# Hybrid trunk kernel: the forget cumulative sums move behind the k projection of the fox branch's first head

## The chip, the cores and the metric

One Trainium2 chip, of which the kernel uses one core. The metric is the device time of one execution in microseconds (us); lower is better. The engines are TensorE (PE in the profile), VectorE (DVE), ScalarE (ACT), GpSimd (POOL) and SyncE (SP), which here issues most DMA transfers. Each engine takes its instructions in the order in which they stand in its own queue, and waits for semaphores that other engines or transfers raise.

## The reference

Two layers over a sequence of 512 rows of width 1024. Each layer is a half-step SwiGLU, then three token mixers in parallel (stick-breaking attention, forgetting attention, cross-attention to a memory of 256 rows), then a second half-step SwiGLU. What matters here is the forgetting ("fox") branch with 8 heads of width 64:

```python
u = _rmsnorm(h, mix_pre_g[l])
proj = u @ w_in[l]
q_sb, k_sb, v_sb, q_fx, k_fx, v_fx, f_logit, q_mem = jnp.split(proj, split_at, axis=-1)
log_f = jax.nn.log_sigmoid((f_logit + b_forget[l]).astype(jnp.float32)).transpose(0, 2, 1)
...
def _forgetting_attention(q, k, v, log_f):
    c = lax.cumsum(log_f.astype(jnp.float32), axis=2)
    ...
        z = jnp.einsum('bhqd,bhkd->bhqk', qb, k).astype(jnp.float32) * scale
        z = z + cb[..., :, None] - c[..., None, :]
        ...softmax over the causal keys, times v
```

So each head's scores get a bias from the running sum `c` of its log forget gates, one number per row and head.

## The kernel before

Matrix products are made of three products of split numbers (`mm3`, lines 205 to 207: high by high, high by low, low by high), 128 x 128 weights against 512 columns, accumulated in PSUM. A weight block is a `Unit`: SP fetches it into a `raw_` buffer (line 249; there are two such buffers), ACT casts the high part `wh_` from it (line 179, or 182 with a scale), DVE subtracts to get the low part `wl_` (line 180 or 183), which frees the raw buffer for the next fetch. There are four places for `wh_` and four for `wl_`. All names below have a layer and head number in the code; the profile leaves the numbers out.

The work of a layer's mixing stage is a queue of jobs (`Q.add`). Each job names the units that it needs, and a generator that issues matmuls piece by piece. When a job begins, its units and at least four of those of the jobs behind it are loaded (`load_ahead`). The attention heads are chains that are woven into the jobs: `weave` issues the pieces of jobs until an assumed time has passed, then the chain's next step. So between the matmuls of the projections stand a head's scores (`zs`, line 1153), its transposes (`pts`, line 1128) and its product with the values (`pvs`, line 1114). The stick-breaking heads come first: between `zs` and `pts`, ACT and DVE make the weights `ts` (lines 1158 to 1168, of which line 1168 is the last exponential on ACT). All instructions of an engine then stand in a fixed order, which a scheduler makes from this program order and its own estimate of times.

PSUM has eight banks in two rings of four. The ring `mm` serves the projections: `pv` (values), `pq` and `pk` (q and k of a pair of heads), `pg` (gates), `pb` (branch products), `pvs`, and `pfl`, which is the bank of the forget sums.

The fox branch begins with the head pair `FOX[0]`, which is pair 2, while the stick-breaking heads of pair 2 still run. Its jobs are:

- `v_gates`: the values of the pair and, in eight more columns, the forget logits. For each of four row tiles PE fills a bank `pv`, ACT and DVE split the values out of it, and DVE copies the eight logit columns to `fl` (line 1334).
- the q projection (`proj`): 24 matmuls into `pq`, then a split by ACT and DVE.
- `forget_cumsum`: PE transposes the four tiles of `fl` into `pfl` (line 1283); ACT and DVE make the log-sigmoid and the running sum (a scan, line 1290); ACT, DVE and POOL place it in four row groups of the tile `cs` (lines 1293 to 1296).
- the k projection: 24 matmuls into `pk`, then a split, and two copies on POOL (line 1362).
- a `merge` job of the memory branch: the gate product `pg`, its sigmoid (lines 193 to 201), the branch product `pb`.

`cs` is read by `fox_pre` (line 1188), which builds the bias operand `qk` of each fox head.

Of the kernel before, what the change touches and what calls it, by code (L numbers as in the profile page):

```python
# [22 lines left out]
def kernel(  # L23
# [1250 lines left out]
    FOX = (2, 3, 0, 1)  # L1274

    def forget_cumsum(l, fl, holder):

        pt = pbank("mm", f"pfl{l}")
        for t in range(NT):
            tc.keep_in_program_order(nc.tensor.transpose(pt[:NH, t * P:(t + 1) * P], fl[:, t], ident[:]))
        yield 0.3
        a, b, y = tmp(f"fa{l}")[:NH], tmp(f"fb{l}")[:NH], bfor[:, l:l + 1]
        nc.scalar.activation(a, pt[:NH], AF.Abs, bias=y)
        nc.scalar.activation(a, a, AF.Exp, scale=-1.0)
        nc.scalar.activation(a, a, AF.Ln, bias=one_t[:NH])
        nc.vector.tensor_scalar(b, pt[:NH], y, 0.0, ALU.add, ALU.min)
        nc.vector.tensor_tensor_scan(b, b, a, 0.0, ALU.add, ALU.subtract)  # L1290
        cs = stile([P, S], "cs", f"cs{l}")
        nc.gpsimd.memset(cs[:].bitcast(F32), 0.0)
        nc.scalar.copy(cs[0:NH], b)
        nc.vector.tensor_tensor(cs[32:32 + NH], b, cs[0:NH].bitcast(F32), ALU.subtract)
        for c in (0, 32):
            nc.gpsimd.tensor_copy(cs[64 + c:64 + c + NH], cs[c:c + NH])
        holder["cs"] = cs

    def mixing(l, src, ks, vs, rest, dst):
# [44 lines left out]
        def proj(key, un, scale):  # L1344
            nm = f"{key[0]}{l}_{key[1]}_{key[2]}"
            pt = pbank("mm", "p" + nm)
            yield from gemm(pt[:], [un], 0, act)
            if key[0] == "q":

                t = st[key] = blk("q", nm)  # L1350
                for r, ro, j in HEAD_ROWS:
                    split(t[r, j], t[ro, j], pt[r], scale=scale)
            else:

                twice = key[1] == 0
                t = st[key] = stile([P, 4 if twice else 3, S], "k", nm)
                for r, ro, j in HEAD_ROWS:
                    split(t[r, j], t[r, 2 + j if twice else 2], pt[r])
                    if twice:
                        nc.gpsimd.tensor_copy(t[ro, j::2], t[r, j::2])  # L1360
                    else:
                        nc.gpsimd.tensor_copy(t[ro, j], t[r, j])
# [12 lines left out]
        def project(br, p):  # L1375
            base = br * 1536
            marks["before", br, p] = len(Q.jobs)
            for x, off, scale in (("q", 0, 0.125), ("k", 512, None)):
                un1 = Unit(w_in[l], 0, ND, base + off + p * P, P, f"{x}{l}_{br}_{p}")
                marks[br, p] = Q.add([un1], lambda x=x, un1=un1, scale=scale: proj((x, br, p), un1, scale))  # L1380
                if (br, p, x) == (1, FOX[0], "q"):
                    Q.add([], lambda: forget_cumsum(l, st["fl"], st))

        def merge(br, w_br, dp, apart=False, saved=False):
# [58 lines left out]

        heads, fox = [(0, p) for p in range(NP)] + [(1, p) for p in FOX], []
        project(*heads[0])
        project_v(*heads[0])
        marks[heads[0]] = len(Q.jobs)
        for i, (br, _) in enumerate(heads):
            if i + 1 < len(heads):
                project(*heads[i + 1])  # L1450
            if br == 0:
                merge(2, w_br_mem, i)
            else:
                merge(0, w_br_sb, i - NP, apart=i == NP)
            if i % 2 == 0 and i + 2 < len(heads):
                project_v(*heads[i + 2])
            if i in (1, 3):
                fox.append(merge(1, w_br_fox, i // 2, True, True))
# [239 lines left out]
```

## Time and profile before

| | |
|---|---|
| time, median of three runs | 2399.95 us (2398.45 to 2400.62) |
| profiled execution: time | 2400.15 us |
| profiled execution: span of the instructions | 2398.4 us |
| PE busy | 2375.6 us, 99% of the span |
| DVE busy | 1862.4 us, 78% |
| ACT busy | 1392.5 us, 58% |
| POOL busy | 78.4 us, 3% |
| DMA | 338.22 MB, mean 141 GB/s |

The span runs from the first to the last instruction; the profiled execution's time has 1.75 us around it. A busy PE is not a PE at its peak: the profile also gives the clock that was granted to it (PEclk), as a share of full speed. In the views a row of the timeline is: start and duration in us, engine, line, operation, tile written <- tiles read, shape, count, and in brackets the idle time of the engine before it and what ended that.

### The profile page before, as it was taken

The page shows a single profiled execution, that of the slowest core. Times are in us where ns is not written, and L with a number is a line of the kernel's source. Part 1 is how long each engine was busy: PE and PEld are TensorE (multiplying, and loading weights), DVE is VectorE, ACT ScalarE, POOL GpSimd, SP SyncE. Part 2 cuts the span into 40 slices and gives each one's busy share as a digit, 9 for nine tenths or more (in the row PEclk, how much of TensorE's full clock was granted, in tenths as well). Part 3 has the DMA queues.
Part 4 walks back from the last instruction along what each step waited for, and adds up shares of the span by engine and source line. Part 5 has one row for each costly group of instructions (what it writes and reads, how often), then busy time and mean ns, then how long its engine had stood idle before and what let it go on. Part 6 is the DMA issues. An engine that isn't in the chain of part 4 may idle for free.

```text
span 2398.4 us, 31561 instructions
## 1 busy us (share of the span) xinstructions
PE 2375.6 (99%) x11975; PEld 2009.8 (84%) x11975; DVE 1862.4 (78%) x2462; ACT 1392.5 (58%) x2201; POOL 78.4 (3%) x134
## 2 busy tenths in 40 slices
PE   9999999999999999999999999999999999999998
PEld 7788889888888888888888888888888888888887
DVE  8878877577777789788788788766667777887885
ACT  6655565576656555555655554655666664655554
POOL 1000000000111000000000000000001100000000
PEclk9999999999999999999999999999999999999999
DMA  5654454222323555544645554532323235555444
GB/s 200 187 150 158 141 194 140 80 82 78 88 80 99 192 181 170 150 150 158 210 138 170 149 175 162 188 107 71 97 71 97 71 122 191 164 182 149 154 139 155
DMA packets 232171, 338.22 MB, mean 141 GB/s; under 512 B 10682, under 2 KB 125394, under 8 KB 232020
## 3 DMA queue, kind: packets, MB, share of 16 engines
q1 hardware_dynamic: 231924, 336.18, 44.3%
q8 instruction: 94, 1.54, 0.3%
q14 instruction: 57, 0.47, 0.1%
q0 software_dynamic: 96, 0.03, 0.0%
HBM read 319.39 MB, written 16.78 MB: 140 GB/s over the span
## 4 chain that ended last, share of the span: by engine, by line
PE 94%; DVE 3%; DMA 1%; ACT 1%; issue 1%; POOL 0%; DVEq 0%; SPq 0%; ACTq 0%
PE pg L206 4%; PE pg L205 4%; PE pg L207 4%; PE pda L206 3%; PE pda L207 3%; PE pda L205 3%; PE pdc L206 3%; PE pdc L207 2%; PE pdc L205 2%; PE pb L207 2%; PE pb L206 2%; PE pb L205 2%; PE pk L205 1%; PE pk L206 1%; PE pk L207 1%; PE pwo L206 1%
## 5 line engine op out<-in xcount | busy, mean ns | idle before, releaser
L205 PE MATMUL pg<-us_a,wh_wg 128*128 128x512 f32 x384 | 150.8, 393 | 0.0
L206 PE MATMUL pg<-us_a,wh_wg 128*128 128x512 f32 x384 | 149.6, 390 | 0.0
L207 PE MATMUL pg<-us_a,wl_wg 128*128 128x512 f32 x384 | 149.6, 390 | 0.0
L206 PE MATMUL pdc<-wl_dc,ahc 128*128 128x512 f32 x224 | 87.6, 391 | 0.1
L206 PE MATMUL pda<-wl_da,aha 128*128 128x512 f32 x224 | 87.6, 391 | 0.0
L205 PE MATMUL pda<-wh_da,aha 128*128 128x512 f32 x224 | 87.4, 390 | 0.0
L205 PE MATMUL pdc<-wh_dc,ahc 128*128 128x512 f32 x224 | 87.4, 390 | 0.0
L207 PE MATMUL pdc<-wh_dc,alc 128*128 128x512 f32 x224 | 87.2, 389 | 0.0
L207 PE MATMUL pda<-wh_da,ala 128*128 128x512 f32 x224 | 87.2, 389 | 0.0
L207 PEld LDWEIGHTS pg<-us_a,wl_wg 128*128 128x128 f32 x384 | 72.1, 188 | 15.2
L205 PEld LDWEIGHTS pg<-us_a,wh_wg 128*128 128x128 f32 x384 | 72.1, 188 | 14.1
L206 PEld LDWEIGHTS pg<-us_a,wh_wg 128*128 128x128 f32 x384 | 72.2, 188 | 14.0
L180 DVE TENSOR_TENSOR wl_dc<-raw_dc,wh_dc 128x1024 fp32r<-128x1024 f32 x50 | 61.2, 1224 | 29.1 <-ACT wh_dc L179 28.5
L180 DVE TENSOR_TENSOR wl_da<-raw_da,wh_da 128x1024 fp32r<-128x1024 f32 x50 | 61.2, 1224 | 22.0 <-ACT wh_da L179 21.7
L179 ACT CAST wh_dc<-raw_dc 128x1024 fp32r<-128x1024 f32 x50 | 52.7, 1054 | 43.8 <-PE pdc L207 14.9
L179 ACT CAST wh_da<-raw_da 128x1024 fp32r<-128x1024 f32 x50 | 52.7, 1054 | 38.7 <-PE pda L207 14.5
L183 DVE SCALAR_TENSOR_TENSOR wl_wg<-raw_wg,wh_wg 128x1024 fp32r<-128x1024 f32 x48 | 58.4, 1221 | 20.4 <-ACT wh_wg L182 20.1
L179 ACT CAST wh_uc<-raw_uc 128x1024 fp32r<-128x1024 f32 x44 | 46.3, 1053 | 41.9 <-PE pwc1u L207 10.3
L182 ACT ACTIVATE wh_wg<-raw_wg 128x1024 fp32r<-128x1024 f32 x48 | 50.6, 1057 | 28.0 <-PE pv L1089 12.6
L179 ACT CAST wh_ua<-raw_ua 128x1024 fp32r<-128x1024 f32 x44 | 46.2, 1052 | 34.5 <-PE pwa1u L207 10.3
L180 DVE TENSOR_TENSOR wl_uc<-raw_uc,wh_uc 128x1024 fp32r<-128x1024 f32 x44 | 53.7, 1221 | 13.0 <-ACT wh_uc L179 12.9
L180 DVE TENSOR_TENSOR wl_ua<-raw_ua,wh_ua 128x1024 fp32r<-128x1024 f32 x44 | 53.6, 1220 | 10.2 <-ACT wh_ua L179 10.2
(654 smaller groups left out, 8028.8 us busy)
## 6 DMA issues: line engine op xcount, KB each, us to landing
raw_da<-in_ffn_w_down_dram SPq DMA_DIRECT2D x66, 512.0 KB, 4.5
raw_dc<-in_ffn_w_down_dram SPq DMA_DIRECT2D x66, 512.0 KB, 4.9
raw_ga<-in_ffn_w_gate_dram SPq DMA_DIRECT2D x52, 512.0 KB, 3.8
raw_ua<-in_ffn_w_up_dram SPq DMA_DIRECT2D x52, 512.0 KB, 3.9
raw_gc<-in_ffn_w_gate_dram SPq DMA_DIRECT2D x52, 512.0 KB, 3.7
raw_uc<-in_ffn_w_up_dram SPq DMA_DIRECT2D x52, 512.0 KB, 3.7
raw_wg<-in_w_gate_dram SPq DMA_DIRECT2D x48, 512.0 KB, 3.5
raw_wo<-in_w_out_dram SPq DMA_DIRECT2D x24, 512.0 KB, 3.6
```

The source lines that it names most:

```text
L179: both = [nc.scalar.copy(h_ap, src)]
L180: make = lambda: nc.vector.tensor_tensor(l_ap, src, h_ap.bitcast(F32), ALU.subtract)
L182: both = [nc.scalar.activation(h_ap, src, AF.Copy, scale=scale)]
L183: make = lambda: nc.vector.scalar_tensor_tensor(l_ap, src, scale, h_ap.bitcast(F32), ALU.mult, ALU.subtract)
L205: nc.tensor.matmul(pt, lh, rh, start=start, stop=False, skip_group_check=free)
L206: nc.tensor.matmul(pt, lh, rl, start=False, stop=False, skip_group_check=free)
L207: nc.tensor.matmul(pt, ll, rh, start=False, stop=stop, skip_group_check=free)
```

## The change

The job `forget_cumsum` of each layer is put into the queue after the k projection of the fox branch's first head pair instead of after its q projection. Computation, tiles and transfers are the same; their order differs.

```diff
             for x, off, scale in (("q", 0, 0.125), ("k", 512, None)):
                 un1 = Unit(w_in[l], 0, ND, base + off + p * P, P, f"{x}{l}_{br}_{p}")
                 marks[br, p] = Q.add([un1], lambda x=x, un1=un1, scale=scale: proj((x, br, p), un1, scale))
-                if (br, p, x) == (1, FOX[0], "q"):
+                if (br, p, x) == (1, FOX[0], "k"):
                     Q.add([], lambda: forget_cumsum(l, st["fl"], st))
```

`marks[br, p]`, the place up to which the queue must have run before the pair's head begins, is taken before that line in both kernels.

## The prediction

> **What bounds the kernel now.** I read the page first: the busy shares, and the chain of work that ended last.
>
> ```profile
> PE 2375.6 (99%) x11975; PEld 2009.8 (84%) x11975; DVE 1862.4 (78%) x2462; ACT 1392.5 (58%) x2201; POOL 78.4 (3%) x134
> ...
> PE 94%; DVE 3%; DMA 1%; ACT 1%; issue 1%; POOL 0%; DVEq 0%; SPq 0%; ACTq 0%
> ```
>
> TensorE (PE) is busy for 99% of the span and is 94% of the chain, so only time in which PE stands still, or runs slowly, can be won. The second view is therefore the waits of PE alone.
>
> ```profile
> engine line waited for: us in total, times, longest us
> PE pfl L1283 <- DVE fl L1334: 9.0, 2, 4.5
> PE warm L1558 <- DVE warm L1650: 1.3, 1, 1.3
> ```
>
> Its longest wait is the one that the change touches: twice, once in each layer, the transposes of the forget logits (`pfl`, line 1283) wait 4.5 us for VectorE's (DVE's) copies of those logits (`fl`, line 1334). The third view is the timeline of the first of the two, engine by engine: PE, then DVE, then ScalarE (ACT).
>
> ```profile
> 577.50 0.39 PE L205 MATMUL pq<-us_a,wh_q 128*128 128x512 f32 x1
> ...
> 582.97 0.38 PE L1283 MATMUL pfl<-ident,fl 128*8 128x128 f32 x2
> 587.87 0.38 PE L1283 MATMUL pfl<-ident,fl 128*8 128x128 f32 x1 [4.52 <-DVE fl L1334]
> 587.90 0.77 PE L205 MATMUL pk<-us_a,wh_k 128*128 128x512 f32 x1
> ...
> 595.08 1.25 PE L1128 MATMUL pts<-ident,ts 128*128 128x128 f32 x10
> 596.09 0.48 PE L205 MATMUL pk<-us_a,wh_k 128*128 128x512 f32 x1
> ...
> 596.86 0.39 PE L205 MATMUL pg<-us_a,wh_wg 128*128 128x512 f32 x1
> ```
> ```profile
> 578.34 1.20 DVE L180 TENSOR_TENSOR wl_k<-raw_k,wh_k 128x1024 fp32r<-128x1024 f32 x1
> ...
> 586.51 1.23 DVE L180 TENSOR_TENSOR wl_wb<-raw_wb,wh_wb 128x1024 fp32r<-128x1024 f32 x1 [0.18 <-ACT wh_wb L179]
> 587.65 0.16 DVE L1334 COPY fl<-pv 128x8 f32<-128x8 f32 x1
> ...
> 588.06 0.16 DVE L1334 COPY fl<-pv 128x8 f32<-128x8 f32 x1
> ```
> ```profile
> 585.43 1.04 ACT L179 CAST wh_wb<-raw_wb 128x1024 fp32r<-128x1024 f32 x1 [0.38 <-DMA raw_wb<-in_w_br_mem_dram]
> 586.38 0.52 ACT L1168 ACTIVATE ts<-ts 128x384 f32<-128x384 f32 x1
> ```
>
> The q projection `pq` ends its issue at 582.97, and two of the four transposes run. The third needs the copy at 587.65. That copy reads a PSUM bank that PE filled long before; it is late because DVE takes its instructions in order and the low part of a weight unit (`wl_wb`, 586.51) stands ahead of it. That one waits for ACT's cast of the unit (585.43), which waits for the unit's transfer, and the chain of waits gives this transfer's own time:
>
> ```profile
> 580.70 4.71 DMA raw_wb<-in_w_br_mem_dram
> ```
>
> So PE stands still for a weight that only a later job needs. The second layer does the same at 1772.10:
>
> ```profile
> 1772.10 0.38 PE L1283 MATMUL pfl<-ident,fl 128*8 128x128 f32 x2
> 1776.93 0.38 PE L1283 MATMUL pfl<-ident,fl 128*8 128x128 f32 x1 [4.46 <-DVE fl L1334]
> ...
> 1785.33 0.39 PE L205 MATMUL pg<-us_a,wh_wg 128*128 128x512 f32 x1
> ```
>
> The fourth view cuts both places into stretches, with the granted clock in the last but two columns.
>
> ```profile
> core 0: us, PE busy (x) PEld busy (x) DVE busy (x) ACT busy (x) POOL busy (x), PEclk, DMA share, GB/s
> ...
> 587.87:596.86 8.99, 8.99 (x36) 7.16 (x37) 5.47 (x10) 4.66 (x10) 1.67 (x2) 0.74 0.32 97
> ...
> 1776.93:1785.33 8.40, 8.40 (x37) 6.76 (x37) 5.47 (x10) 4.67 (x10) 1.66 (x2) 0.80 0.34 105
> ```
>
> Behind each standstill PE is busy without a gap, but its mean granted clock is 0.74 and 0.80. The k projection pays for the wait a second time.
>
> **The change part by part.** It moves the whole job `forget_cumsum` behind the k projection in the queue. Nothing is added or removed.
>
> PE. In the built order of the changed program the 24 matmuls of `pk` follow `pq` directly, then come the ten transposes `pts`, then all four `pfl`, then `pg`. Can `pk` start at 582.97? It needs a PSUM bank: it takes the one that `pfl` had, and since two `pfl` ran at 582.97, that bank was free. It needs its weights: `wl_k`, the later of the two parts, ended at 578.34 + 1.20 = 579.54. So nothing holds it. The 24 matmuls of `pq` took 582.97 - 577.50 = 5.47 us at the full clock, and 24 of `pk` take the same: 588.44. `pts` needs the last exponential, over at 586.38 + 0.52 = 586.90; its cost is 596.09 - 595.08 = 1.01, so 589.45. `pfl` needs the last `fl` copy, over at 588.06 + 0.16 = 588.22. This is the cover that counts: the copies are as late as before, but the k projection and `pts` now hide them, with 1.23 us to spare. Four `pfl` at some 0.11 us each (ten `pts` transposes in 1.01, nearly the same shape) end at 589.9, and `pg` starts there instead of at 596.86: 6.96 us won. In the second layer the same 6.93 us of work leads from 1772.10 to 1779.03 instead of 1785.33: 6.30 us. The sum is 13.3 us. Of it 4.52 + 4.46 = 9.0 us is standstill, and the other 4.3 us is nearly all the low clock.
>
> On this clock the Trainium skill ("TensorE: Matmul & The Clock Gate", Part 1, "What's actually happening") says that an idle window of about 3.4 us halves the clock and a busy window of about 3.4 us restores it, with windows that run freely. By that rule alone each standstill costs 1.7 us more, and the sum would be an estimated 12.4 us. The trace agrees on the kind (4.5 us idle, then a low clock) and gives 0.9 us more in all.
>
> DVE, ACT and POOL. The job's own chain (three activations, two DVE steps and a scan, one cast, two POOL copies) keeps its place relative to `pfl` and so comes some 2 us later than before. Its result `cs` is read much later, as the first of these rows (the tile `cs` as a whole) shows; some 45 us of room hide it:
>
> ```profile
> L1188 DVE TENSOR_SCALAR qk<-cs,sel x16: 457/481/669, 641.3 to 1947.0; 40x512 fp32r<-40x512 f32 x8, 64x512 fp32r<-64x512 f32 x8
> L1296 POOL CAST cs<-cs x4: 608/831/1057, 594.1 to 1784.3; 8x512 fp32r<-8x512 f32 x4
> ```
>
> POOL's order changes only in that its two k copies come ahead of the `cs` copies. The job issues no DMA. SP's queue here keeps the order of its weight transfers.
>
> What is late next. The seven idle microseconds were also time in which ACT and DVE caught up. In the built order the job's chain now meets the gate and attention chains of the following job, and ACT casts the next k unit (`wh_k`) *ahead* of the last exponential (line 1168) that the next `pts` needs. In the profile of before the exponential comes first:
>
> ```profile
> 615.71 0.51 ACT L1168 ACTIVATE ts<-ts 128x384 f32<-128x384 f32 x1
> 616.13 0.67 ACT L193 ACTIVATE ga<-pg,nbgate 128x512 f32<-128x512 f32 x1
> 617.46 1.05 ACT L179 CAST wh_k<-raw_k 128x1024 fp32r<-128x1024 f32 x1 [0.66 <-DMA raw_k<-in_w_in_dram]
> ```
> ```profile
> 603.59 0.62 PE L1153 MATMUL zs<-k,q 128*128 128x512 f32 x2
> ...
> 612.41 1.22 DVE L183 SCALAR_TENSOR_TENSOR wl_wg<-raw_wg,wh_wg 128x1024 fp32r<-128x1024 f32 x1
> ...
> 613.66 0.37 SPq L249 DMA_DIRECT2D raw_k<-in_w_in_dram  x1
> ...
> 619.17 1.25 PE L1128 MATMUL pts<-ident,ts 128*128 128x128 f32 x10
> ```
>
> So a wait is added: the last exponential, and behind it PE's `pts`, stand behind the transfer `raw_k`, which SP may start only when `wl_wg` (612.41) has freed its place. Before, `raw_k` was issued 613.66 - 603.59 = 10.07 us after the scores `zs` began. In the changed order `zs` begins at 589.9 + (603.59 - 596.86) + 0.68 (three matmuls of `pb` come ahead of it) = 597.3, so the issue is at 607.4 at best. The transfer takes 617.46 - 613.66 = 3.80, the cast 1.05, the exponential 0.51: 612.8. PE reaches those transposes 619.17 - 596.86 + 0.68 = 22.99 us after `pg`, at 612.9. That is even at best; with a step or two of the job's displaced chain (0.6 to 0.7 us each on ACT or DVE) ahead of `wl_wg`, PE waits. I take 0.5 us per layer, between 0 and 1.5. Below nothing it cannot be, since PE has no idle time there now to win.
>
> The sum: 13.3 - 1.0 = 12.3 us. The profiled execution took 2400.15 us, of which 2398.4 is the span; the 1.75 us around it stay. It lies 0.2 us above the median of the three runs (2399.95, from 2398.45 to 2400.62). 2400.15 - 12.3 = 2387.9 us.
>
> **The rivals.** *Partly given back.* The wait at `pts`, or one at the moved `pfl` (1.23 us of room behind a transfer that took 4.71), is longer than I take, but shorter than the 4.5 us that are seen to cost clock. For it speaks that both stand behind transfers; against it, that this stage's transfers, 3.80 and 4.71 us, are priced already. With up to 3.3 us per layer: 2386.9 + 6.6 = 2393.5 us at most. Chance 0.14.
>
> *It does not do what it says.* Something else than `fl` holds PE until 587.65, and `pk` inherits the wait: a bank, or a weight. Then PE stands as before, and the time is 2400 us. Against it: the rows for `wl_k` and for the two `pfl` at 582.97. Chance 0.05.
>
> *Slower.* The transfer `raw_k` becomes the bound of the stage: ACT stands behind it, then `pts`, then the whole next head. It loses more than was won from a wait of 4.5 us per layer on, because a standstill of that length is seen to bring the low clock with it (6.3 to 7.0 us each); that needs a transfer of 8 us. It is slower by 0.2%, that is over 2405 us, with some 9 us, of which 7 stand and 2 are clock; at 7.5 us of standstill it gives 2386.9 + 2 x 9.5 = 2406 us. The order of ACT's queue speaks for it, the two transfer times against it. Chance 0.04.
>
> **How the numbers follow.** The forecast, 2387.9 us, has the remaining 0.77, and lies between 2386.9 (no new wait) and 2389.9 (1.5 us per layer), to which run-to-run scatter of 1.7 us below the profiled execution is added: 2385.2. The range from 2385.0 to 2393.5 takes in the first rival and leaves out 0.09 of named cases. About 0.2%, 4.8 us, is what a measurement of this kernel can tell from no change; faster than that (under 2395.1) are the forecast and the first rival, 0.91; the second rival is the same, 0.05; the third is slower, 0.04.
>
> **What would show it.** In the profile of the changed kernel the wait of `pfl` on `fl` is gone from PE's waits, `pk` runs in some 5.5 us at a granted clock of 1.0, and `pg` follows `pq` after some 6.9 us in both layers. A new line `pts` behind line 1168, of up to a microsecond or so, is the term that I am least sure of. I am wrong if `pk`'s first matmul shows the old wait, if any PE wait of over 3.3 us appears in the heads behind it, or if the granted clock still drops there.

## The result and the profile after

The changed kernel takes 2388.56 us (median of four executions, 2386.77 to 2389.78) where the kernel before takes 2400.28 us on the same chip (2398.45 to 2400.86): a ratio of 0.9953, with a 95% interval from 0.9938 to 0.9968. Run again later on another chip it took 2390.96 us against 2401.22 us: 0.9956, from 0.9944 to 0.9969. That is 11.7 us won the first time and 10.3 the second. The forecast was 2387.9 us, in a range from 2385.0 to 2393.5. The profiled execution took 2388.54 us, 2386.8 us of it the span. One execution of experiment 4 below took 11399 us and is left out of its ratio.

From the page after, the busy shares and the chain of work that ended last:

```profile
PE 2370.1 (99%) x11975; PEld 2007.1 (84%) x11975; DVE 1862.3 (78%) x2462; ACT 1392.1 (58%) x2201; POOL 74.9 (3%) x134
...
PE 91%; DVE 4%; DMA 2%; ACT 1%; issue 1%; SPq 0%; POOL 0%; DVEq 0%; ACTq 0%
```

The counts of instructions are the same. What is new is in the chain: three points less of PE, one more each of DVE and of the transfers (the shares are rounded). The waits of PE say where (us in total, times, longest):

```profile
PE pts L1128 <- ACT ts L1168: 1.5, 2, 0.9
```

The 9.0 us at `pfl` are gone; in their place stand 1.5 us at `pts`, once in each layer. The timeline of PE in the first layer, then that of DVE and ACT:

```profile
582.23 0.39 PE L205 MATMUL pk<-us_a,wh_k 128*128 128x512 f32 x1
...
587.68 1.26 PE L1128 MATMUL pts<-ident,ts 128*128 128x128 f32 x10
588.77 0.60 PE L1283 MATMUL pfl<-ident,fl 128*8 128x128 f32 x4
...
612.23 0.49 PE L1128 MATMUL pts<-ident,ts 128*128 128x128 f32 x3
613.27 0.98 PE L1128 MATMUL pts<-ident,ts 128*128 128x128 f32 x7 [0.55 <-ACT ts L1168]
```
```profile
585.50 1.22 DVE L180 TENSOR_TENSOR wl_wb<-raw_wb,wh_wb 128x1024 fp32r<-128x1024 f32 x1
...
587.04 0.16 DVE L1334 COPY fl<-pv 128x8 f32<-128x8 f32 x1
...
611.75 1.05 ACT L179 CAST wh_k<-raw_k 128x1024 fp32r<-128x1024 f32 x1 [2.13 <-DMA raw_k<-in_w_in_dram]
612.70 0.52 ACT L1168 ACTIVATE ts<-ts 128x384 f32<-128x384 f32 x1
```

The copies `fl` come as late as before, behind `wl_wb` on DVE, but PE now does `pk` and ten `pts` in the meantime and needs the last copy only at 588.77, 1.57 us after it is done. Further on, ACT casts `wh_k`, for whose transfer it waited 2.13 us, ahead of the exponential, and PE waits 0.55 us for that. In the second layer the same wait is 0.94 us:

```profile
1796.93 0.98 PE L1128 MATMUL pts<-ident,ts 128*128 128x128 f32 x7 [0.94 <-ACT ts L1168]
```

Cut into stretches, from the first `pk` to the first `pg` in either layer (busy time of each engine, then the granted clock):

```profile
582.23:589.13 6.90, 6.90 (x39) 5.82 (x38) 6.21 (x13) 4.67 (x7) 0.00 (x0) 1.00 0.55 167
1765.51:1772.41 6.90, 6.90 (x40) 5.82 (x38) 5.75 (x13) 4.03 (x7) 0.00 (x0) 1.00 0.55 167
```

Both take 6.90 us at a clock of 1.00, where the way from the end of `pq` to `pg` took 13.89 and 13.23 us. So 6.99 + 6.33 = 13.3 us are won and 1.5 lost: 11.8 us. The spans differ by 2398.4 - 2386.8 = 11.6 us.

### The profile page after: what moved, and what is told of

The parts are those of the page before. It is cut to its first block, busy times and chain, and to the rows that moved or that the text cites. A ratio compares the mean times of both kernels' runs of the same rounds, so it can differ in the third digit from the quotient of the medians.

```text
span 2386.8 us, 31552 instructions
## 1 busy us (share of the span) xinstructions
PE 2370.1 (99%) x11975; PEld 2007.1 (84%) x11975; DVE 1862.3 (78%) x2462; ACT 1392.1 (58%) x2201; POOL 74.9 (3%) x134
## 4 chain that ended last, share of the span: by engine, by line
PE 91%; DVE 4%; DMA 2%; ACT 1%; issue 1%; SPq 0%; POOL 0%; DVEq 0%; ACTq 0%
PE pg L206 3%; PE pg L207 3%; PE pg L205 3%; PE pda L206 3%; PE pda L207 3%; PE pda L205 3%; PE pdc L206 2%; PE pdc L207 2%; PE pdc L205 2%; PE pb L207 2%; PE pb L206 2%; PE pb L205 2%; PE pq L205 1%; PE pq L207 1%; PE pq L206 1%; PE pwo L207 1%
## 5 line engine op out<-in xcount | busy, mean ns | idle before, releaser
L179 ACT CAST wh_uc<-raw_uc 128x1024 fp32r<-128x1024 f32 x44 | 46.3, 1053 | 39.6 <-PE pwc0u L207 10.3
L179 ACT CAST wh_ua<-raw_ua 128x1024 fp32r<-128x1024 f32 x44 | 46.2, 1052 | 34.5 <-PE pwa1u L207 10.3
L182 ACT ACTIVATE wh_wg<-raw_wg 128x1024 fp32r<-128x1024 f32 x48 | 50.4, 1054 | 23.7 <-PE pv L1089 11.7
L180 DVE TENSOR_TENSOR wl_uc<-raw_uc,wh_uc 128x1024 fp32r<-128x1024 f32 x44 | 53.7, 1221 | 11.8 <-ACT wh_uc L179 11.7
```

Of the source, the lines that this page charges most:

```text
L179: both = [nc.scalar.copy(h_ap, src)]
L180: make = lambda: nc.vector.tensor_tensor(l_ap, src, h_ap.bitcast(F32), ALU.subtract)
L182: both = [nc.scalar.activation(h_ap, src, AF.Copy, scale=scale)]
```

## The experiments

The runs 1 to 4 share one chip, on which the kernel before takes 2400.67 us; the runs 5 to 8 share another, with 2401.22 us.

**1. The move in the first layer alone.**

```diff
-                if (br, p, x) == (1, FOX[0], "k"):
+                if (br, p, x) == (1, FOX[0], "k" if l == 0 else "q"):
```

> The move is made in the first layer alone. Theory (each layer pays its own standstill and its own low clock, and the move wins both there): the first layer wins 6.9 us and gets a wait of about 0.5 us at its `pts`, the second keeps its wait of 4.46 us at `pfl` and its low clock. 2400.3 - 6.4 = 2393.9 us. Rival (the gain comes from one of the layers alone, or from a rearrangement further on): 2400 or 2388.5 us.

Measured: 2396.55 us, the median of eleven executions from 2392.89 to 2401.09, a ratio of 0.9981 (0.9973 to 0.9990), 4.1 us won instead of 6.4. Waits of PE, and the stretches first `pk` to `pg` of layer 0 and third `pfl` to `pg` of layer 1:

```profile
PE pfl L1283 <- DVE fl L1334: 4.4, 1, 4.4
PE pts L1128 <- ACT ts L1168: 1.9, 1, 1.9
...
583.18:590.08 6.90, 6.90 (x40) 5.82 (x38) 5.52 (x12) 3.43 (x5) 0.00 (x0) 1.00 0.47 146
...
1772.61:1781.90 9.29, 9.29 (x36) 7.41 (x37) 5.48 (x10) 4.66 (x10) 1.67 (x2) 0.71 0.30 98
```

Each layer does pay for itself: the moved one takes 6.90 us again, the other keeps its standstill and its low clock. The size is off in two terms of the profiled execution (2397.05 us). The wait at `pts` is 1.86 us where I took 0.5, and the low clock of the second layer cost 9.29 us of stretch instead of the 8.40 in the profile before, with the same standstill of 4.4 us. Together that is 2.2 us, about what is missing; with executions that lie up to 8 us apart the close fit to 2.3 is luck.

**2. Only the copies to `fl` on another engine,** the sums at their old place.

```diff
-                nc.vector.tensor_copy(st["fl"][:, t], pt[:, 4 * HD:4 * HD + NH])
+                nc.scalar.copy(st["fl"][:, t], pt[:, 4 * HD:4 * HD + NH])
```

> The sums stay where they were in the kernel before; only the copy of the forget logits to `fl` is moved from DVE to ACT. Theory (PE stood still because the copies queued on DVE behind the weight unit `wl_wb` and its transfer; the place of the sums in the job queue has nothing to do with it): in the built order the third copy comes on ACT right behind the cast `wh_wg` at about 584, so the third `pfl` waits about 1 us in each layer instead of 4.5, too short to lower the granted clock as before. 13.3 us won, 2.3 lost: about 2389.5 us. Rival (the copies are not the cause; the gain is in what follows the new place, the order of the k projection and the gates): about 2400 us, since that order is as before.

Measured: 2390.06 us, a ratio of 0.9954 (0.9941 to 0.9966). The first row of PE's waits:

```profile
PE pfl L1283 <- ACT fl L1334: 2.3, 3, 1.1
```

13.3 - 2.3 = 11.0 forecast, 10.6 measured, with the order of the jobs untouched. So the cause of the standstill is the place of the copies on DVE, behind a weight that a later job needs, and moving the sums is one of several ways around it. The longest of the three waits, 1.09 us, is that of the second layer's third transpose, at 1768.41. Around it, from 1765 to 1780, the granted clock is 1.00 (third number from the right); a wait of about a microsecond brought no low clock:

```profile
1765.00:1780.00 15.00, 13.91 (x69) 11.13 (x68) 13.74 (x22) 10.18 (x20) 2.35 (x2) 1.00 0.45 139
```

**3. The standstill filled with products that nobody needs.**

```diff
+        for _ in range(20):
+            tc.keep_in_program_order(nc.tensor.matmul(pt[:], u[:, 0, 0, 0:P], u[:, 0, 0, :], start=True, stop=True))
```

> The kernel before, with 20 more matmuls of 128x512 in each layer, put ahead of the four transposes, into the same PSUM bank, whose values are then overwritten by the transposes. They cost no path of their own, since PE would stand still for 4.5 us there: 20 x 0.227 = 4.54 us. They keep PE busy and so tell the standstill from the clock behind it. Theory (about 4.3 us of the 13.3 are the low granted clock behind the standstills): the standstill stays, the clock does not drop, 2400.3 - 4.0 = 2396.3 us, and the stretch from the last `pfl` to `pg` takes 6.9 us at a clock of 1.0. Rival (the clock's column is not worth time, the 4.3 us are something else): 2400.3 us or a little more, and the stretch still takes 8.4 to 9.0 us.

Measured: 2401.91 us, a ratio of 1.0002 (0.9993 to 1.0011). The total missed its forecast by 5.6 us. The stretches from the first `pk` to `pg` in the two layers, then the row of the first layer's wait:

```profile
589.68:597.97 8.29, 8.29 (x36) 6.78 (x37) 5.09 (x8) 4.67 (x10) 1.67 (x2) 0.79 0.19 63
...
1781.65:1788.31 6.66, 6.66 (x36) 5.65 (x37) 4.59 (x8) 4.62 (x10) 1.18 (x2) 1.00 0.34 101
```
```profile
589.25 0.68 PE L1285 MATMUL pfl<-ident,fl 128*8 128x128 f32 x2 [1.85 <-DVE fl L1336]
```

In the second layer it went as the theory says: the fillers take the standstill, the clock stays at 1.00, and the matmuls from the first `pk` to `pg` take 6.66 us. In the profile before they take, with one transpose `pfl` among them, 8.37 us in that layer and 8.96 in the first:

```profile
587.90:596.86 8.96, 8.96 (x36) 7.13 (x37) 5.44 (x10) 4.66 (x10) 1.67 (x2) 0.74 0.31 96
1776.96:1785.33 8.37, 8.37 (x37) 6.73 (x37) 5.44 (x10) 4.67 (x10) 1.66 (x2) 0.80 0.34 105
```

So the low clock cost 8.96 - 6.66 = 2.3 us and 8.37 - 6.66 = 1.7 us, 4.0 of the 4.3 us that the prediction put down to it. In the first layer the transfer `raw_wb` took 6.57 us, so that the copies came after the fillers, PE still waited 1.85 us, and the low clock came back after that. It told nothing apart there. The profiled execution (2404.06 us) lies 7.8 us above the forecast. From the end of `pq` to `pg` its first layer took 15.49 us (from 582.48) instead of 13.89, and its second 12.06 (from 1776.25) instead of 13.23: 0.4 us lost where 4.0 were forecast to be won. Waits of 1.0 to 1.6 us at `pwo`, `utc` and `pdc` make 3.3 us more than in the profile before, in stages whose order of instructions is unchanged; where they come from stays open, and the total of this run supports no theory.

**4. The last exponential ahead of the cast `wh_k`,** in the kernel after. The exponential and the cast are kept in the program's order, and the job of the gate `wg` ahead of them loads only three units in advance instead of four, so that the k unit and its cast come one job later in the program, behind the exponential. The diff shows only the exponential's part:

```diff
-            nc.scalar.activation(t[:, :w], t[:, :w], AF.Exp)
+            ex = nc.scalar.activation(t[:, :w], t[:, :w], AF.Exp)
+            if name[0] == "s" and name[2:] == "_3_0":
+                tc.keep_in_program_order(ex)
```

> The kernel after, with ACT's last exponential of the following stick-breaking head (line 1168) put back ahead of the cast of the next k unit, `wh_k`, in both layers (to that end one more unit is loaded ahead at the start of the job behind). Theory (the new wait of 0.55 and 0.94 us at `pts` is that exponential standing behind the cast, which waits for its transfer): the wait goes, 2388.6 - 1.5 = about 2387.1 us. Rival (the exponential itself is late because its input from DVE is late, since the displaced chain of the sums stands there): the wait stays, 2388.6 us or more.

Measured: 2388.91 us, a ratio of 0.9950 (0.9936 to 0.9964): 11.8 us won, as much as the kernel after won beside its own runs of before (11.7). ACT, then PE in the first layer:

```profile
614.22 0.52 ACT L1169 ACTIVATE ts<-ts 128x384 f32<-128x384 f32 x1 [2.06 <-DVE ts L1168]
```
```profile
614.79 0.98 PE L1129 MATMUL pts<-ident,ts 128*128 128x128 f32 x7 [0.81 <-ACT ts L1169]
```

The wait is gone in the second layer, where all ten transposes run at once at 1796.06. In the first 0.81 us stay although no transfer stands ahead of the exponential any more: now the exponential waits for its own input from DVE. Theory and rival are each half right, so something behind both is late. The next run's chain shows it.

**5. The kernel after again,** beside the runs 6 to 8, nothing changed.

> The kernel after again, beside the three others on the same chip. Both theories: 2388.6 us, a ratio of 0.995 to the kernel before, with a scatter of one or two us from the transfer `raw_wb`, which took from 4.4 to 6.6 us in the profiles so far.

Measured: 2390.96 us, 0.9956 (0.9944 to 0.9969). PE waits 1.9 us at `pts`, 1.13 of it in the first layer. The chain of waits that ends there (start, duration, what), with the pieces between left out:

```profile
581.00 4.57 DMA raw_wb<-in_w_br_mem_dram
...
586.67 1.23 DVE wl_wb L180
...
592.71 0.56 ACT fa L1286
...
597.29 0.62 ACT cs L1293
...
608.07 1.13 DVE wl_wg L183
609.22 4.07 DMA raw_k<-in_w_in_dram
...
613.37 1.04 ACT wh_k L179
614.41 0.43 ACT ts L1168
```

From the transfer `raw_wb` at 581 to `pts` at 615 ACT and DVE hand work to each other without a pause, and the moved sums (from `fa` to `cs`) are in the middle of it. If this is the cause, the wait can be worked out for a run from where `wl_wb` starts, how long `raw_k` takes, and when PE comes to `pts`. The rows of the kernel after and of run 1 (chain of waits) that this needs:

```profile
608.04 3.63 DMA raw_k<-in_w_in_dram
```
```profile
580.90 5.86 DMA raw_wb<-in_w_br_mem_dram
587.87 1.23 DVE wl_wb L180
...
610.41 3.66 DMA raw_k<-in_w_in_dram
```
```profile
613.32 0.49 PE L1128 MATMUL pts<-ident,ts 128*128 128x128 f32 x3
615.66 0.98 PE L1128 MATMUL pts<-ident,ts 128*128 128x128 f32 x7 [1.86 <-ACT ts L1168]
```

Run 1 against the kernel after: `wl_wb` 587.87 - 585.50 = 2.37 us later, PE 613.32 - 612.23 = 1.09 later, `raw_k` 0.03 longer: 0.55 + 2.37 - 1.09 + 0.03 = 1.86 us; measured 1.86. This run: 1.17 us later, PE 1.04 later, `raw_k` 4.07 - 3.63 = 0.44 longer: 1.12 us; measured 1.13. The second layers fit too: in the kernel after `wl_wb` starts at 1769.32, PE comes at 1795.51 and `raw_k` takes 3.47, which gives 0.93 us for the 0.94 measured; in this run 1769.97, 1796.49 and 3.67 give 0.80 for 0.79. In this order of instructions the wait at `pts` thus carries, one for one, whatever `wl_wb` is late. A late `raw_wb` is not needed for it: in the first layer of the kernel after ACT cast `wh_wb` at 584.39 without waiting for the transfer, `wl_wb` stood behind DVE's own work, and 0.55 us were left all the same.

**6. The sums one job further back,** behind the `merge` job. The `if` of the diff goes out of the loop, and at the end of the branch's last gate job stands:

```diff
+                if i == NP - 1:
+                    Q.add([], lambda: forget_cumsum(l, st["fl"], st))
```

> The sums are put one job further back, behind the `merge` job of the memory branch (gates `pg`, branch products `pb`). Theory (the wait at `pts` is the end of one chain that ACT and DVE run back to back: transfer `raw_wb`, `wl_wb`, the copies `fl`, the split of q, `wh_wg`, the casts of `pts`, the split of k, the sums' own activations and scan, the gates, `ts`, `wl_wg`, transfer `raw_k`, `wh_k`, exponential; the sums take about 3.3 us of it, from 593.5 to 596.8 in the profile after): with the sums out of it the wait of 1.5 us in all is gone although ACT still casts `wh_k` ahead of the exponential: 2388.6 - 1.5 = about 2387.1 us. Rival (the wait is the transfer `raw_k` and the order of ACT alone, which stay): it stays at 0.5 to 2 us a layer, 2388.6 us. Second rival (the sums, now late, hold up the following heads): over 2390 us.

Measured: 2387.12 us (2385.96 to 2388.47), a ratio of 0.9941 (0.9928 to 0.9953). Neither `pfl` nor `pts` is among PE's waits. ACT, then PE in the first layer:

```profile
611.47 1.05 ACT L179 CAST wh_k<-raw_k 128x1024 fp32r<-128x1024 f32 x1 [2.32 <-DMA raw_k<-in_w_in_dram]
612.42 0.52 ACT L1168 ACTIVATE ts<-ts 128x384 f32<-128x384 f32 x1
```
```profile
612.58 1.40 PE L1128 MATMUL pts<-ident,ts 128*128 128x128 f32 x10
```

ACT still casts `wh_k` ahead of the exponential, and here `raw_wb` was late (ACT waited 2.01 us for it and cast `wh_wb` at 587.16), yet PE goes through `pts` without a wait. So the order of ACT alone isn't the cause. What changed is the length of the chain, from `wl_wb` to the `wl_wg` that frees the place for `raw_k`; DVE in this run, then in the kernel after:

```profile
588.24 1.23 DVE L180 TENSOR_TENSOR wl_wb<-raw_wb,wh_wb 128x1024 fp32r<-128x1024 f32 x1 [1.72 <-ACT wh_wb L179]
...
606.34 1.20 DVE L183 SCALAR_TENSOR_TENSOR wl_wg<-raw_wg,wh_wg 128x1024 fp32r<-128x1024 f32 x1
```
```profile
606.81 1.20 DVE L183 SCALAR_TENSOR_TENSOR wl_wg<-raw_wg,wh_wg 128x1024 fp32r<-128x1024 f32 x1
```

It is 606.81 - 585.50 = 21.31 us with the sums (21.31 in run 1 and 21.32 in run 5 too) and 606.34 - 588.24 = 18.10 without: the sums are 3.2 us of it. By the reckoning of run 5, the times of this run with the longer chain would have given a wait of some 3.1 us. So the margin is thin: the ten transposes take 1.40 us instead of 1.26. Against run 5 on the same chip this run takes 3.8 us less, and the executions of the two do not overlap (run 5: 2389.40 to 2392.29). The waits at `pts` account for 1.9 us of it; another microsecond is waits in stages that the change doesn't touch (`pwo` 0.5, `pdc` 0.3 and `pda` 0.2 us in run 5), and the rest isn't found.

**7. The copies early on ACT,** the sums at their old place: the copy of run 2, written ahead of the cast of the values.

```diff
+                nc.scalar.copy(st["fl"][:, t], pt[:, 4 * HD:4 * HD + NH])
                 e = 2 * (t % 2)
...
-                nc.vector.tensor_copy(st["fl"][:, t], pt[:, 4 * HD:4 * HD + NH])
```

> The sums stay where they were before; the copy of the logits to `fl` goes to ACT and is written ahead of the cast of the values from the same bank, so that in the built order the last two copies stand directly ahead of those casts (at about 580 and 581), before the q projection ends at 583. In the built order ACT's last exponential stays ahead of `wh_k` too, and the sums' chain comes during the k projection. Theory (the copies' place behind `wl_wb` on DVE is the whole cause; with early copies neither the standstill nor the new wait at `pts` is there): 2400.4 - 13.3 = about 2387.1 us, no wait at `pfl` and none at `pts`. Rival (two small copies and the sums on ACT at this point delay the exponentials or the splits as much as the move does): 2388.5 to 2390 us.

Measured: 2388.22 us (2387.47 to 2389.09), a ratio of 0.9946 (0.9934 to 0.9959). PE in the first layer:

```profile
582.48 0.60 PE L1283 MATMUL pfl<-ident,fl 128*8 128x128 f32 x4
```

The last copy is over at 580.44, all four transposes run at once, and there is no wait at `pfl` and none at `pts`, in either layer. The theory's picture holds. The time is 1.1 us above its number, which was taken from a kernel before at 2400.4 us; beside its own runs of before (2401.22) 13.0 us are won, of the 13.3 forecast.

**8. `raw_wb` fetched twice** in the kernel after, to make it late.

```diff
-            nc.sync.dma_start(self.raw[:], self.src[self.k0 * P:(self.k0 + self.nk) * P, self.c0:self.c0 + self.ncol]
+            for _ in range(2 if self.name in ("wb0_2_3_0", "wb1_2_3_0") else 1):
+                nc.sync.dma_start(self.raw[:], self.src[self.k0 * P:(self.k0 + self.nk) * P, self.c0:self.c0 + self.ncol]
```

> The kernel after, in which the weight block that stands ahead of the copies `fl` (`raw_wb` of the first merge unit) is fetched twice in each layer, one after the other, so that it lands about 4.4 us later. Nothing else is changed. Theory (the k projection only covers the copies, with 0.1 to 1.6 us to spare, and all that follows on ACT and DVE hangs on the same transfer): `pfl` waits some 3 us in each layer and `pts` more than before, together about 4.4 us a layer, some of it shared with a low clock: 2388.6 + 8.8 = about 2397.4 us. Rival (behind the k projection nothing hangs on that transfer any more, the move has taken it off the path): 2388.6 us. Second rival (only `pfl` waits, and what comes behind makes it up): 2388.6 + 2 x 3.2 = 2395 us.

Measured: 2389.55 us, a ratio of 0.9952 (0.9938 to 0.9965), nothing of the 8.8 us. DVE in the first layer:

```profile
586.52 0.16 DVE L1335 COPY fl<-pv 128x8 f32<-128x8 f32 x1
...
591.09 1.23 DVE L180 TENSOR_TENSOR wl_wb<-raw_wb,wh_wb 128x1024 fp32r<-128x1024 f32 x1 [2.35 <-ACT wh_wb L179]
```

The scheduler expects the second fetch and puts the copies and the split of q ahead of `wl_wb`. So this isn't the kernel after with a late weight, and the forecast isn't tested. What it does show agrees with run 2: with the copies ahead of it, the weight came at 590 and `pfl` didn't wait. `pts` did, 1.6 us in all (0.78 and 0.79 in the two layers), so `wl_wb` was 5.6 us later than in the kernel after for about the same wait. The reckoning of run 5 doesn't carry over to this order, in which the exponential stands ahead of the cast `wh_k` and waits for DVE, as in run 4.

## Why the prediction was right, point by point

*Standstill and cover.* Right. `pfl` waits for nothing, `pk` takes 582.23 to 587.68, 5.45 us, and the way to `pg` is 6.90 us (6.93 forecast). That `fl` on DVE was the cause is shown by run 2, which removes it without any move. The cover of 1.23 us is not a constant: it was 1.57 us in the kernel after, but in run 1, where `raw_wb` took 5.86 us, the last copy ended at 589.58 and `pfl` began at 589.72:

```profile
589.42 0.16 DVE L1334 COPY fl<-pv 128x8 f32<-128x8 f32 x1
```
```profile
589.72 0.60 PE L1283 MATMUL pfl<-ident,fl 128*8 128x128 f32 x4
```

The move hides the copies just so; the runs 6 and 7 do it with room.

*The low clock.* Right in size: 4.3 us forecast, 4.0 by the stretches of run 3 with the layer where the fillers held as the measure. By the rule of the Trainium skill that the prediction cites ("TensorE: Matmul & The Clock Gate", Part 1, "What's actually happening") it would be an estimated 3.4 us. What failed is a side remark, that only standstills of 4.5 us are seen to cost clock (it bounded the first rival): see below.

*The new wait.* The mechanism was named, the size missed: 0.55 + 0.94 = 1.5 us, 1.9 in run 5 and 1.86 in one layer of run 1, where 1.0 was taken, and single layers go beyond the end of 1.5. The step that failed is the reckoning of the issue of `raw_k` from the start of `zs`, with "a step or two of the job's displaced chain" added. The rows that show it are the start of `zs` and ACT's first step on it, in the kernel after, and that step in the kernel before, where `zs` began at 603.59:

```profile
596.65 1.44 PE L1153 MATMUL zs<-k,q 128*128 128x512 f32 x8
```
```profile
599.60 0.60 ACT L1158 ACTIVATE ts<-zs 128x512 f32<-128x512 f32 x1
```
```profile
604.45 0.98 ACT L1158 ACTIVATE ts<-zs 128x512 f32<-128x512 f32 x2
```

Before, ACT took up the scores 0.86 us after `zs` began; now it takes 2.95, and `raw_k` goes out 608.04 - 596.65 = 11.39 us after `zs` instead of 10.07. ACT and DVE come into that place late already, out of the chain from `wl_wb`, of which the sums are 3.2 us (run 6). In the first comparison the larger wait makes 0.5 of the 0.66 us by which the time lies above the forecast, a difference that is smaller than the scatter of the four executions.

*`cs`, POOL, SP.* No wait for `cs` shows up among PE's in any run.

*The rivals.* Partly given back: in kind, yes, but 1.5 us in all and not 6.6. That the move doesn't do what it says is excluded by the rows of `pk`, and by run 1, where the layer that isn't moved stays as it was. That `raw_k` becomes the bound was not seen: it stands in the chain that ends at `pts`, but it took 3.5 to 4.1 us there, far from the 8 us at which it would decide.

## What to carry to other kernels

Where PE waits for a small copy, look at what stands ahead of that copy in its engine's queue: here a weight split that waits for a transfer, and the simplest cure is to put the copy ahead of it, on another engine (run 7). Moving the consumer works too, but only as well as the work that moves with it finds room: behind the k projection it left 1.5 to 1.9 us of waits, one job further back none (run 6, whose executions overlap with those of run 7). When a stall is removed, follow the displaced work through the engines that had caught up during the stall: here a chain without a pause on two engines passed a late transfer on to PE (runs 1 and 5). A place that looks covered by a microsecond should be read in several profiles: the room ahead of `pfl` was 1.57 us in one and 0.14 in another.

## What the runs showed of the hardware that was not expected

A standstill doesn't have one price in clock. The granted clock is halved in stretches that can be cut out of the traces (length, PE busy, and the clock as the third number from the right); the kernel before, then run 1, then run 3:

```profile
585.69:592.51 6.82, 4.64 (x12) 3.48 (x13) 4.88 (x10) 3.83 (x6) 0.00 (x0) 0.50 0.51 156
...
1776.94:1780.35 3.41, 3.41 (x10) 2.52 (x11) 2.22 (x5) 1.89 (x3) 0.00 (x0) 0.50 0.83 258
```
```profile
1771.09:1777.92 6.83, 5.31 (x14) 4.03 (x15) 5.00 (x9) 3.26 (x6) 0.00 (x0) 0.50 0.50 154
```
```profile
590.47:593.88 3.41, 3.41 (x10) 2.64 (x9) 2.23 (x3) 2.49 (x4) 0.00 (x0) 0.50 0.41 142
```

Each is 3.41 us long or twice that, and it costs half of the time that PE works in it: 2.3 and 1.7 us behind the standstills of 4.52 and 4.46 us, 2.7 behind the one of 4.41 us in run 1, and 1.7 behind one of only 1.85 us in run 3. Taken as the stretch from `pk` to `pg` beyond the 6.66 us of run 3, the costs are 2.3, 1.7, 2.6 and 1.6 us. The low clock doesn't begin with the standstill either: in run 3 PE had been at work again for 1.2 us (from 589.25) when it came. In the 3.41 us ahead of these four stretches PE was busy for 1.07, 0.01, 0.52 and 1.43 us; the wait of 1.09 us in run 2 brought no low clock.

The Trainium skill ("TensorE: Matmul & The Clock Gate", Part 1, "What's actually happening") has windows of about 3.4 us that run freely; the lengths and the starting points of these stretches agree with that. It asks for an idle window of 3.4 us, though, and here 3.41 us in which PE was still busy for 1.43, with a standstill of 1.85, were enough.

The same transfer of 512 KB (`raw_wb`) took 4.57 us in run 5, 4.71 in the kernel before, 5.86 in run 1 and 6.57 in run 3, in a place where the cover is about as much as they differ. These are profiles of different kernels; why it varies is open.
